# The opening of a hybrid decoder layer in another order: residual stream and query products first, memory tokens after them

## The chip, the cores and the metric

One core of one Trainium2 chip. The time is device microseconds of one execution of the whole kernel; lower is better. The kernel before took 2308.29 us, the median of three runs (2306.86 to 2318.2).

## The reference, cut to what matters

One layer on 512 tokens of width 2048, in float32. The change touches only what comes first: the embedding layer norm, a few columns of the input projection (gates, forget logits, the queries of the memory heads), and the keys and values of 256 memory tokens.

```
h = layer_norm(x, emb_ln_g, emb_ln_b)                 # x: 512 x 2048
proj = h @ w_in                                       # all heads' columns
moba_qkv, nsa_q, nsa_kv, nsa_g, fox_qkv, fox_f, mem_q = split(proj)
gates = sigmoid(nsa_g);  log_f = log_sigmoid(fox_f + b_forget)
ek, ev = split(mem @ w_mem_kv)                        # mem: 256 x 2048, 4 heads of 64 each
o_mem = softmax(mem_q @ ek.T / 8) @ ev
...                                                   # 28 more heads, output projection,
...                                                   # layer norm, gated MLP, layer norm
```

## The kernel before, in words

Every float32 product is made from two parts: an operand is rounded to a shorter type (the high part, by ScalarE) and the rest is kept as a low part (by VectorE, a subtraction). A product is then three matmuls: high by high, high by low, low by high (`PARTS`, line 118). All weights of a projection come in units of 128 x 1024 (512 KB): `load_unit` (line 88) loads one into a raw slot (tag `wr`, 4 slots), `nc.scalar.copy` makes the high part (line 99, tag `wh`, 2 slots) and `nc.vector.tensor_sub` the low part (line 100, tag `wl`, 2 slots). A tile of 128 output columns takes two units, that is 16 steps of 128 rows (`kt`) with three matmuls each (`gemm_t`, line 123).

The order of the instructions of each engine is written by a scheduler that follows the order of the program and moves an instruction up where its inputs are there. `high_priority(offset=n)` lets it act as if the instruction stood n places earlier; `self.ahead = 900` (line 1325) gives that to all units loaded after it. Attention of earlier heads is put into a queue and one stage of it is taken up by `tick` (line 141) for each so many columns of matmuls in `gemm_t`; `first_products` of the change does not count columns.

`build` (line 1293) opens in this order. The constants are made, and ScalarE's queue loads `prm` (line 182), a table of scales and offsets. The queue of SyncE (SP) then loads the memory tokens (`load_mem`, four tiles of 512 KB in tag `T`), the units of `w_mem_kv` and the residual stream x (`ln0_load`, sixteen tiles of 256 KB), mixed. `split_mem` splits the memory tokens; `mem_kv` makes four tiles of memory keys and values (tile `mkv`, 48 matmuls of 256 columns each, two units each), and between them `ln0_tile` normalises one token tile of x: `bn_stats` on VectorE (line 229), aggregation (lines 202 to 204), a power on GpSimd (line 205, engine POOL), the scale `nb` (line 233) and the normalisation itself, half on GpSimd (line 236), half on ScalarE (line 239).

`ln0_transpose` (line 241) then turns x: 4 transposes of 128 x 128 on TensorE per `kt` into a PSUM bank, and `evac_T` (line 208) takes it out by ScalarE (line 213, tile `ev`), GpSimd (the high part, line 215) and VectorE (the low part, line 216). The result, 16 tiles `T` of 128 x 1024, uses all 16 slots of tag `T`; in the kernel before the memory tokens, raw and split, hold 12 of these slots until the memory products are done. `fg` (line 425) makes gates and forget logits: its small weights are split side by side into one tile, so a `kt` takes two matmuls of 512 columns (line 437). `memory` (line 508) makes the two tiles of memory queries (`mq`, line 131) and queues the four memory heads. `fox` (first tile `fq`) follows.

`fg_stages` (line 443) is the first queued item. Its first stage is a chain of small steps on VectorE and ScalarE (lines 446 to 470), with two loads of ScalarE's function table, six GpSimd memsets and twelve small DMAs on SP's queue (line 478).

Of the kernel before, what the change touches and what calls it, by code (L numbers as in the profile page):

```python
# [11 lines left out]
F32 = mybir.dt.float32  # L12
F32R = mybir.dt.float32r
# [4 lines left out]
P = 128  # L18
S = 512
D = 2048  # L20
KT = D // P
NT = S // P
NMEM = 256
# [18 lines left out]
class Trunk:  # L42
# [176 lines left out]
    def ln0_load(self, t):  # L219
        self.xs.append([self.tmp(f"x{t}{n}") for n in range(4)])  # L220
        for n in range(4):
            self.nc.sync.dma_start(self.xs[t][n], self.x[t * P:(t + 1) * P, n * 512:(n + 1) * 512])

    def ln0_tile(self, t):
        nc = self.nc
# [196 lines left out]
        self.bias.append(b)  # L422


    def fg(self):

        nc = self.nc
        ps = self.bank("g", "fg")
        for u in range(2):
            raw = self.pW.tile([P, 8, 64], F32, tag="wr", name="wr", bufs=4)  # L430
            nc.sync.dma_start(raw, self.wfg[u])
            w = self.pW.tile([P, 8, P], F32R, tag="wh", name="wh", bufs=2)
            nc.scalar.copy(w[:, :, 0:64], raw)
            nc.vector.tensor_sub(w[:, :, 64:128], raw, w[:, :, 0:64].bitcast(F32))
            for k in range(8):
                for b in range(2):
                    nc.tensor.matmul(ps, w[:, k], self.xT_part(8 * u + k, b),
                                     start=(u + k + b == 0), stop=(u == 1 and k == 7 and b == 1))
        self.gates = self.cst.tile([P, NT, 24], F32, name="gates")
        self.crow = []  # L440
        self.queue.append(self.fg_stages(ps))

    def fg_stages(self, ps):
        nc = self.nc
# [47 lines left out]


    def load_mem(self, c):
        raw = self.pT.tile([P, 4, NMEM], F32, tag="T", name="mraw")
        self.nc.sync.dma_start(raw, self.memt[:, 4 * c:4 * c + 4, :])
        self.mraw.append(raw)

    def split_mem(self):
        for raw in self.mraw:  # L500
            h, l = (self.pT.tile([P, 4, NMEM], F32R, tag="T", name="mem") for _ in range(2))
            self.split_pair(raw, h, l)
            self.mt.append((h, l))

    def mem_kv(self, m, units):
        part = lambda kt, b: self.mt[kt // 4][b][:, kt % 4, :]
        ps = self.gemm_t(None, part, N=NMEM, units=units, name="mkv")
        return (self.stack_k if m < 2 else self.make_v)(ps, NMEM)

    def memory(self, kv):  # L510
        for c in range(2):
            qs = self.stack_q(self.wm_tile("mq"))
            oT = self.new_oT(14 + c)
            for h2 in range(2):
                self.queue.append(self.mem_head(qs[h2], kv[c][h2], kv[2 + c], h2, oT))
# [776 lines left out]

    def build(self):
        self.oT, self.bias = {}, []
        self.constants()

        self.xs, self.mraw, self.mt, kv = [], [], [], []
        unit = lambda m, u: self.load_unit(self.wmkv[m, u])

        def units(m, ahead):  # L1300
            with self.tc.high_priority(offset=ahead):
                return [unit(m, u) for u in range(2)]

        u0 = []
        for u in range(2):
            self.load_mem(2 * u)
            u0.append(unit(0, u))
            self.load_mem(2 * u + 1)
        self.ln0_load(0)
        u1 = units(1, 0)  # L1310
        for t in range(1, NT):
            self.ln0_load(t)
        self.split_mem()
        kv.append(self.mem_kv(0, u0))
        self.ln0_tile(0)
        u2 = units(2, 80)
        kv.append(self.mem_kv(1, u1))
        self.ln0_tile(1)
        self.ln0_tile(2)
        u3 = units(3, 0)  # L1320
        kv.append(self.mem_kv(2, u2))
        self.ln0_tile(3)
        kv.append(self.mem_kv(3, u3))
        self.ln0_transpose()
        self.ahead = 900
        self.fg()
        self.memory(kv)
        self.every = 23
        self.fox()
        self.every = 10  # L1330
        self.nsa_setup()
        for p in range(4):
            self.nsa_pair(p)
            self.moba_pair(p)
        self.out_proj()
        self.ffn()
# [91 lines left out]
```

## Time and profile before

| | |
|---|---|
| median of three runs | 2308.29 us |
| the profiled execution | 2307.26 us |
| its span, first to last instruction | 2305.2 us |
| TensorE (PE) matmuls busy | 2222.3 us, 96% |
| VectorE (DVE) | 1549.5 us, 67% |
| ScalarE (ACT) | 1234.9 us, 54% |
| GpSimd (POOL) | 1337.1 us, 58% |
| bytes by DMA | 392.74 MB, mean 170 GB/s |

The profile shows one execution. A busy share is the time in which an engine has an instruction in hand; matmuls overlap their neighbours, so the distance from start to start tells more of their rate than the duration. Times in rows are in us, means of groups in ns; "idle before" is the engine's idle time just ahead of these instructions and the arrow names what ended it. PEld is the loading of weights into TensorE; SPq and ACTq are the queues from which SyncE and ScalarE issue DMAs.

### The profile page before, as it was taken

The page shows a single profiled execution, that of the slowest core. Times are in us where ns is not written, and L with a number is a line of the kernel's source. Part 1 is how long each engine was busy: PE and PEld are TensorE (multiplying, and loading weights), DVE is VectorE, ACT ScalarE, POOL GpSimd, SP SyncE. Part 2 cuts the span into 40 slices and gives each one's busy share as a digit, 9 for nine tenths or more (in the row PEclk, how much of TensorE's full clock was granted, in tenths as well). Part 3 has the DMA queues.
Part 4 walks back from the last instruction along what each step waited for, and adds up shares of the span by engine and source line. Part 5 has one row for each costly group of instructions (what it writes and reads, how often), then busy time and mean ns, then how long its engine had stood idle before and what let it go on. Part 6 is the DMA issues. An engine that isn't in the chain of part 4 may idle for free. (4 is left out here: it accounts for less than half of the span.)

```text
span 2305.2 us, 40383 instructions
## 1 busy us (share of the span) xinstructions
PE 2222.3 (96%) x15454; PEld 2075.7 (90%) x15454; DVE 1549.5 (67%) x2212; ACT 1234.9 (54%) x2131; POOL 1337.1 (58%) x1199
## 2 busy tenths in 40 slices
PE   7999999999999998999999999999999899999995
PEld 6788888888888887899999999999999899999994
DVE  7544455466675338677776776776666987797878
ACT  5444443355564235665566566566656565665641
POOL 5212110133224706878787877888778677777675
PEclk9999999999999999999999999999999999999997
DMA  6322223221223453888888888888888888887963
GB/s 232 94 77 80 74 73 101 83 64 56 72 81 107 144 160 116 206 228 227 221 231 231 222 228 207 223 231 221 214 202 234 256 238 219 204 234 189 256 171 108
DMA packets 125362, 392.74 MB, mean 170 GB/s; under 512 B 13633, under 2 KB 23745, under 8 KB 125169
## 3 DMA queue, kind: packets, MB, share of 16 engines
q1 hardware_dynamic: 106304, 287.72, 37.6%
q0 software_dynamic: 18720, 102.24, 24.7%
q8 instruction: 121, 1.98, 0.3%
q14 instruction: 73, 0.59, 0.1%
q10 hardware_dynamic: 144, 0.21, 0.0%
HBM read 354.36 MB, written 35.65 MB: 169 GB/s over the span
## 5 line engine op out<-in xcount | busy, mean ns | idle before, releaser
L900 DVE TENSOR_TENSOR ws<-S,ws 128x512 fp32r<-128x512 f32 x512 | 621.5, 1233 | 245.6 <-ACT ws L899 242.3
L899 ACT CAST ws<-S 128x512 fp32r<-128x512 f32 x512 | 314.2, 614 | 140.2 <-PE up L977 57.9
L977 PE MATMUL up<-xt,ws 128*128 128x256 f32 x3096 | 386.4, 283 | 0.1
L977 PEld LDWEIGHTS up<-xt,ws 128*128 128x128 f32 x3096 | 378.0, 192 | 0.3 <-DVE ws L900 0.3
L100 DVE TENSOR_TENSOR wl<-wr,wh 128x1024 fp32r<-128x1024 f32 x122 | 154.7, 1268 | 213.7 <-ACT wh L99 192.1
L942 ACT CAST wh<-wr 128x512 fp32r<-128x512 f32 (+1 forms) x260 | 211.8, 831 | 136.8 <-PE up L977 135.0
L950 POOL TENSOR_TENSOR S<-wr 128x512 f32<-128x512 f32 x128 | 203.1, 1587 | 111.7 <-DVE ws L900 106.2
L342 POOL TENSOR_SCALAR P<-P,r 128x128 f32<-128x128 f32 (+3 forms) x144 | 81.2, 582 | 308.5 <-DVE r L337 166.1
L99 ACT CAST wh<-wr 128x1024 fp32r<-128x1024 f32 x122 | 128.0, 1049 | 236.1 <-PE op L733 78.7
L977 PE MATMUL up<-x,wh 128*128 128x256 f32 x1376 | 253.4, 284 | 0.0
L948 POOL TENSOR_TENSOR S<-wr 128x512 f32<-128x512 f32 x128 | 178.7, 1396 | 112.1 <-issue 68.4
L939 ACT ACTIVATE wl<-wr 128x512 fp32r<-128x512 f32 (+1 forms) x260 | 205.3, 837 | 66.8 <-PE dn L1154 55.6
L977 PEld LDWEIGHTS up<-x,wh 128*128 128x128 f32 x1376 | 216.2, 193 | 0.0
L951 POOL TENSOR_TENSOR S<-wr,S 128x512 f32<-128x512 f32 x128 | 212.1, 1657 | 0.0
L977 PE MATMUL up<-x,wl 128*128 128x256 f32 x688 | 196.3, 285 | 6.3 <-DMA wl<-in_wup_dram 6.3
L949 POOL TENSOR_TENSOR S<-S,wr 128x512 f32<-128x512 f32 x128 | 186.8, 1459 | 9.8
L1154 PE MATMUL dn<-wh,hx 128*128 128x256 f32 x792 | 158.3, 293 | 14.6 <-DVE acc L1167 5.9
L1154 PEld LDWEIGHTS dn<-wh,hx 128*128 128x128 f32 x792 | 132.6, 201 | 16.1 <-issue 6.4
L733 PE MATMUL op<-wh,oTs 128*128 128x512 f32 x448 | 140.7, 391 | 0.0
L977 PEld LDWEIGHTS up<-x,wl 128*128 128x128 f32 x688 | 133.1, 193 | 7.3 <-DMA wl<-in_wup_dram 7.3
L977 PE MATMUL up<-x,ws 128*128 128x256 f32 x1032 | 137.9, 283 | 0.0
L1154 PE MATMUL dn<-ws,hx 128*128 128x256 f32 x1044 | 134.1, 285 | 0.1
(331 smaller groups left out, 5143.3 us busy)
## 6 DMA issues: line engine op xcount, KB each, us to landing
wr<-in_wup_dram SPq DMA_DIRECT2D x176, 512.0 KB
wl<-in_wup_dram POOLq DMA_DIRECT2D x88, 768.0 KB, 7.4
wr<-in_wm_dram SPq DMA_DIRECT2D x84, 512.0 KB
wr<-in_wdown_dram SPq DMA_DIRECT2D x84, 512.0 KB
wl<-in_wdown_dram POOLq DMA_DIRECT2D x42, 768.0 KB, 7.8
wr<-in_wout_dram SPq DMA_DIRECT2D x32, 512.0 KB
hid<-c SPq DMA_DIRECT2D x44, 256.0 KB
hid<-ht SPq DMA_DIRECT2D x44, 256.0 KB
```

The lines of the kernel that those rows point to most:

```text
L100: nc.vector.tensor_sub(l[:, :cols], raw[:, :cols], h[:, :cols].bitcast(F32))
L733: nc.tensor.matmul(ps, ot[ct][:, a, t * P:(t + 1) * P], w[b][:, c2 * 512:(c2 + 1) * 512], start=(first and (a, b) == (0, 0)), stop=(last a ...
L899: ins = self.nc.scalar.copy(h, raw)
L900: self.nc.vector.tensor_sub(l, raw, h.bitcast(F32))
L939: nc.scalar.mul(l3[:, o], i, -1.0)
L942: nc.scalar.copy(h3[:, o], i)
L948: nc.gpsimd.tensor_add(s12[:, 0], a21, a22)
L949: nc.gpsimd.tensor_sub(s12[:, 1], s12[:, 0], a11)
L950: nc.gpsimd.tensor_sub(s34[:, 0], a11, a21)
L951: nc.gpsimd.tensor_sub(s34[:, 1], a12, s12[:, 1])
L977: self.nc.tensor.matmul(ps, w[iw][i][:, k * P:(k + 1) * P], x[j][ix], start=(opens and k == 0 and (i, j) == (0, 0)), stop=(last and k == 3 ...
L1154: self.nc.tensor.matmul(bk[i][:, a * 256:(a + 1) * 256], x[ix][j][:, a * P:(a + 1) * P], w[iw][p][:, q * 256:(q + 1) * 256], start=first a ...
```

## The change

The residual stream is loaded ahead of all, its sixteen tiles by turns on SP's and on ScalarE's queue. The constants follow, then the gate weights (`fg_weights`, now in four tiles of tag `w`, split from two raw slots) and the two units of the first query tile. All of x is normalised and turned, and `first_products` makes gates (two matmuls) and the first query tile (three) together, step by step. Only then the memory tokens are loaded, into raw weight slots (tag `wr`), split into sixteen small tiles of tag `t` in place of eight in tag `T`, and multiplied; the second query tile follows.

```
     def ln0_load(self, t):
         for n in range(4):
-            self.nc.sync.dma_start(self.xs[t][n], self.x[...])
+            eng = self.nc.scalar if n % 2 else self.nc.sync
+            eng.dma_start(self.xs[t][n], self.x[...])

-    def fg(self):
...
+    def fg_weights(self):
+        out = []
         for u in range(2):
             raw = self.pW.tile([P, 8, 64], F32, tag="wr", name="wr", bufs=4)
             nc.sync.dma_start(raw, self.wfg[u])
+            for i in (0, 4):
+                w = self.tmp("wfg", (P, 4, P), F32R, tag="w")
+                nc.scalar.copy(w[:, :, 0:64], raw[:, i:i + 4])
+                nc.vector.tensor_sub(w[:, :, 64:128], raw[:, i:i + 4],
+                                     w[:, :, 0:64].bitcast(F32))
+                out.append(w)
+        return out
+
+    def first_products(self, wfg, units):
+        pf, pq = self.bank("g", "fg"), self.bank("g", "gt")
+        for kt in range(KT):
+            for b in range(2):
+                nc.tensor.matmul(pf, wfg[kt // 4][:, kt % 4], self.xT_part(kt, b), ...)
+            u, k = divmod(kt, KT // 2)
+            for a, b in self.PARTS:
+                nc.tensor.matmul(pq, units[u][a][:, k * P:(k + 1) * P], self.xT_part(kt, b), ...)
+        self.wm_next = 1
         self.gates = self.cst.tile([P, NT, 24], F32, name="gates")
         self.crow = []
-        self.queue.append(self.fg_stages(ps))
+        self.queue.append(self.fg_stages(pf))
+        return self.stack_q(pq)

     def load_mem(self, c):
-        raw = self.pT.tile([P, 4, NMEM], F32, tag="T", name="mraw")
+        raw = self.pW.tile([P, 4, NMEM], F32, tag="wr", name="mraw", bufs=4)
         self.nc.sync.dma_start(raw, self.memt[:, 4 * c:4 * c + 4, :])
...
+        for i in (0, 2):
+            h, l = (self.tmp("mem", (P, 2, NMEM), F32R) for _ in range(2))
+            self.split_pair(raw[:, i:i + 2], h, l)
             self.mt.append((h, l))

-    def memory(self, kv):
+    def memory(self, kv, first):
         for c in range(2):
-            qs = self.stack_q(self.wm_tile("mq"))
+            qs = self.stack_q(self.wm_tile("mq")) if c else first
...
     def build(self):
+        for t in range(NT):
+            self.ln0_load(t)
         self.constants()
-        ...
+        wfg = self.fg_weights()
+        first = [self.load_unit(self.wm[0, u]) for u in range(2)]
+        for t in range(NT):
+            self.ln0_tile(t)
         self.ln0_transpose()
+        qs = self.first_products(wfg, first)
+        units = []
+        for c in range(4):
+            self.load_mem(c)
+            if c in (1, 3):
+                units.append(self.load_unit(self.wmkv[0, c // 2]))
+        kv = [self.mem_kv(0, units)]
+        for m in range(1, 4):
+            kv.append(self.mem_kv(m, [self.load_unit(self.wmkv[m, u]) for u in range(2)]))
         self.ahead = 900
-        self.fg()
-        self.memory(kv)
+        self.memory(kv, qs)
```

## Rows read from the trace of the kernel before

**Rows 1.** Stretches of the span: us, each engine's busy time, granted clock, DMA share, GB/s.
```profile
0.00:62.00 62.00, 45.28 (x291) 38.15 (x292) 46.23 (x74) 34.43 (x48) 31.58 (x41) 1.00 0.60 216
...
84.00:200.00 116.00, 115.95 (x565) 97.30 (x565) 61.67 (x108) 55.89 (x118) 26.18 (x44) 1.00 0.26 78
```

**Rows 2.** What TensorE waited for, first 62 us: total, times, longest.
```profile
PE mkv L131 <- ACT mem L899: 9.3, 1, 9.3
...
PE mkv L131 <- DVE wl L100: 2.7, 4, 1.2
...
PE mkv L131 <- ACT wh L99: 0.7, 1, 0.7
```

**Rows 3.** Order of time on TensorE: start, duration, instructions, idle before.
```profile
14.31 0.41 PE L131 MATMUL mkv<-mem,wl 128*128 128x256 f32 x1
...
14.95 0.41 PE L131 MATMUL mkv<-mem,wl 128*128 128x256 f32 x1
...
41.24 0.28 PE L131 MATMUL mkv<-mem,wl 128*128 128x256 f32 x1
...
41.60 0.28 PE L131 MATMUL mkv<-mem,wl 128*128 128x256 f32 x1
...
47.94 0.60 PE L174 MATMUL xTp<-ident,x 128*128 128x128 f32 x4
...
48.62 0.60 PE L174 MATMUL xTp<-ident,x 128*128 128x128 f32 x4
...
61.77 0.63 PE L131 MATMUL mq<-T,wh 128*128 128x512 f32 x2
...
83.83 0.62 PE L131 MATMUL fq<-T,wh 128*128 128x512 f32 x2
```

**Rows 4.** The first 28 us in two stretches, columns as in rows 1.
```profile
0.00:6.00 6.00, 0.00 (x0) 0.00 (x0) 0.33 (x6) 1.28 (x1) 3.91 (x13) 1.00 0.63 185
6.00:28.00 22.00, 16.32 (x109) 15.42 (x110) 18.55 (x30) 13.15 (x15) 6.09 (x6) 1.00 1.04 401
```

**Rows 5.** Groups by shape, first 62 us: count, busy us, mean ns, idle before.
```profile
L229 DVE BATCH_NORM_STATS2 st<-x 128x6 f32<-128x512 f32 x16 | 10.4, 678 | 0.1
...
L205 POOL TENSOR_TENSOR mu<-mu,mhalf 128x1 f32<-128x1 f32 x4 | 3.1, 779 | 22.5 <-DVE mu L204 22.3 <-DMA x<-in_x_dram 0.3
...
L236 POOL TENSOR_SCALAR x<-x,mu 128x512 f32<-128x512 f32 x8 | 9.0, 1135 | 0.4
...
L239 ACT ACTIVATE x<-x,nb,mu 128x512 f32<-128x512 f32 x8 | 6.1, 809 | 5.4 <-DVE nb L233 5.4
...
L202 DVE BATCH_NORM_AGGREGATE mv<-st 128x2 f32<-128x24 f32 x4 | 1.0, 257 | 0.0
...
L215 POOL TENSOR_SCALAR T<-ev 128x512 fp32r<-128x512 f32 x16 | 15.6, 999 | 3.9 <-ACT ev L213 3.9
...
L216 DVE TENSOR_TENSOR T<-ev,T 128x512 fp32r<-128x512 f32 x16 | 15.7, 1041 | 1.5 <-POOL T L215 1.5
...
L100 DVE TENSOR_TENSOR wl<-wr,wh 128x1024 fp32r<-128x1024 f32 x9 | 11.0, 1223 | 7.4 <-ACT wh L99 7.4
...
L99 ACT CAST wh<-wr 128x1024 fp32r<-128x1024 f32 x10 | 10.5, 1046 | 17.9 <-DMA wr<-in_wmkv_dram 10.4 <-PE fg L437 7.5
```

**Rows 6.** Order of time on SP's queue: the last raw slots, and the gate chain's DMAs.
```profile
26.64 4.65 SPq L431 DMA_DIRECT2D wr<-in_wfg_dram  x2
36.08 53.44 SPq L93 DMA_DIRECT2D wr<-in_wm_dram  x10
...
98.62 1.49 SPq L478 DMA_DIRECT2D crow<-cn  x2
```

**Rows 7.** Issues of x on SP's queue: ns min/median/max, first and last start.
```profile
L222 SPq DMA_DIRECT2D x<-in_x_dram x16: 327/328/480, 4.1 to 22.3; - x16
```

**Rows 8.** The gate chain's stretch, 77.22 to 92.40 us, columns as in rows 1.
```profile
77.22:92.40 15.18, 15.18 (x68) 12.57 (x68) 10.95 (x16) 8.45 (x10) 3.82 (x8) 1.00 0.29 92
```

**Rows 9.** Groups of VectorE in that stretch: the unit subtractions among them.
```profile
L100 DVE TENSOR_TENSOR wl<-wr,wh 128x1024 fp32r<-128x1024 f32 x3 | 3.6, 1193 | 0.0
```

More of the change, by code (lines that the diff above doesn't have):

```diff
@@ L221, in ln0_load @@
         for n in range(4):
-            self.nc.sync.dma_start(self.xs[t][n], self.x[t * P:(t + 1) * P, n * 512:(n + 1) * 512])
+            eng = self.nc.scalar if n % 2 else self.nc.sync
+            eng.dma_start(self.xs[t][n], self.x[t * P:(t + 1) * P, n * 512:(n + 1) * 512])
     def ln0_tile(self, t):
@@ L422, in alibi @@
         self.bias.append(b)
-    def fg(self):
+    def fg_weights(self):
         nc = self.nc
-        ps = self.bank("g", "fg")
+        out = []
         for u in range(2):
@@ L431, in fg @@
             nc.sync.dma_start(raw, self.wfg[u])
[L432 to L438, printed above, removed]
+            for i in (0, 4):
[6 more added lines that the diff above has]
+    def first_products(self, wfg, units):
+        nc = self.nc
+        pf, pq = self.bank("g", "fg"), self.bank("g", "gt")
+        for kt in range(KT):
+            for b in range(2):
+                nc.tensor.matmul(pf, wfg[kt // 4][:, kt % 4], self.xT_part(kt, b),
+                                 start=(kt + b == 0), stop=(kt == KT - 1 and b == 1))
+            u, k = divmod(kt, KT // 2)
+            for a, b in self.PARTS:
+                nc.tensor.matmul(pq, units[u][a][:, k * P:(k + 1) * P], self.xT_part(kt, b),
+                                 start=(kt == 0 and (a, b) == (0, 0)),
+                                 stop=(kt == KT - 1 and (a, b) == (1, 0)))
+        self.wm_next = 1
         self.gates = self.cst.tile([P, NT, 24], F32, name="gates")
         self.crow = []
-        self.queue.append(self.fg_stages(ps))
+        self.queue.append(self.fg_stages(pf))
+        return self.stack_q(pq)
     def fg_stages(self, ps):
@@ L494, in load_mem @@
     def load_mem(self, c):
-        raw = self.pT.tile([P, 4, NMEM], F32, tag="T", name="mraw")
+        raw = self.pW.tile([P, 4, NMEM], F32, tag="wr", name="mraw", bufs=4)
         self.nc.sync.dma_start(raw, self.memt[:, 4 * c:4 * c + 4, :])
[L497 to L502, printed above, removed]
+        for i in (0, 2):
+            h, l = (self.tmp("mem", (P, 2, NMEM), F32R) for _ in range(2))
+            self.split_pair(raw[:, i:i + 2], h, l)
             self.mt.append((h, l))
     def mem_kv(self, m, units):
-        part = lambda kt, b: self.mt[kt // 4][b][:, kt % 4, :]
+        part = lambda kt, b: self.mt[kt // 2][b][:, kt % 2, :]
         ps = self.gemm_t(None, part, N=NMEM, units=units, name="mkv")
         return (self.stack_k if m < 2 else self.make_v)(ps, NMEM)
-    def memory(self, kv):
+    def memory(self, kv, first):
         for c in range(2):
-            qs = self.stack_q(self.wm_tile("mq"))
+            qs = self.stack_q(self.wm_tile("mq")) if c else first
             oT = self.new_oT(14 + c)
@@ L1294, in build @@
         self.oT, self.bias = {}, []
+        self.xs, self.mt = [], []
+        for t in range(NT):
+            self.ln0_load(t)
         self.constants()
[L1297 to L1323, printed above, removed]
-        self.ln0_transpose()
+        wfg = self.fg_weights()
+        first = [self.load_unit(self.wm[0, u]) for u in range(2)]
+        for t in range(NT):
+            self.ln0_tile(t)
+        self.ln0_transpose()
+        qs = self.first_products(wfg, first)
[7 more added lines that the diff above has]
+            kv.append(self.mem_kv(m, [self.load_unit(self.wmkv[m, u]) for u in range(2)]))
         self.ahead = 900
-        self.fg()
-        self.memory(kv)
+        self.memory(kv, qs)
         self.every = 23
```

## The prediction, made before the changed kernel was run

> **What bounds the kernel now.** I read the stretches of the span first [rows 1]. After the opening's 62 us the matmuls fill nearly every microsecond (115.95 of 116.00 from 84 to 200 us). The change moves no instruction that lies behind the first `fq` tile, and it adds or drops no matmul. So whatever it brings is brought before that tile's first matmul, at 83.83 us [rows 3]; later stages shift as a block. Of these two stretches the opening is the one with holes: 45.28 of 62.00 us.
>
> What TensorE waits for there comes next [rows 2]: 9.3 us until the first memory product can start, 2.7 and 0.7 us between weight units of the memory products. A hole need not be a wait, though, so the order of time is read too [rows 3]. Three numbers come out of it. Three memory matmuls of 256 columns take 0.64 us early on (14.31 to 14.95) and 0.36 us later (41.24 to 41.60): 768 columns at the 1.2 GHz level first, near the 2.4 GHz level after, although the granted-clock column reads 1.00 throughout; the full pace came after 14.95, some 6 us behind the first product at 9.3. A round of four transposes and one gate matmul takes 0.68 us (47.94 to 48.62). And 96 query matmuls take 22.06 us (61.77 to 83.83, two small transposes among them), 0.23 us each or 10.9 us a tile. Between 41.6 and 61.77 us TensorE waits on the making of the `T` tiles: GpSimd 999 ns and VectorE 1041 ns a tile, in step with each other [rows 5].
>
> **The change, part by part.** I follow TensorE from the start to the first `fq` matmul and compare with 83.83 us.
>
> *When x is there.* x is 512 x 2048 x 4 bytes, 4.19 MB. The first 6 us move 6 x 185 KB = 1.1 MB, and then 401 GB/s flow [rows 4], so x is all in at 6 + 3.1/0.401 = 13.7 us, and I take 14.0 with its completion. ScalarE issues eight of the loads, at 0.33 us each [rows 7] 2.6 us, ahead of its `prm` load; it has nothing else to do before the first token tile is measured. SP's sixteen issues, 5.2 us of work, were spread from 4.1 to 22.3 us [rows 7]: an issue can be held by transfers ahead of it. If ScalarE's are, it is held until some 10 us, when only the first token tile waits for it, for 2 to 3 us. I cost that at nothing, since the last tile sets the end. `prm` is needed at 18 us and has 4 us to spare.
>
> SP's queue, nearly alone, holds the DMA engines at a share of 1.04 from 6 us on, but at 0.63 before that [rows 4]. If a second queue filled that ramp from 2 us on, x would be in at 2 + 4.19/0.401 = 12.4 us, 1.3 us sooner; if not, 13.7. I take the latter, since at 0.33 us an issue [rows 7] SP alone puts out 256 KB tiles at 0.8 MB a us, twice what flows. The Trainium skill, "DMA: Bandwidth & Descriptors", section "Issuing engines are not separate DMA queues", says that issuing from several engines saves only the time to issue; by that rule the sum stays as I have it, by the other reading it is 1.3 us less.
>
> *When the transposes start.* After the last load come two `bn_stats` (2 x 0.68), an aggregation (0.26), the power (0.78), three steps on one or two columns (0.2 each by my estimate, below the aggregation) and ScalarE's normalisation (0.81) [rows 5]: 3.8 us, so 17.8. GpSimd has two normalisations of 1.1 and a power for each token tile, near 3.1 us a tile against 2.6 us of loading, so it runs late, and the splits of the gate weights and the first query units are on the same engines: I take **18.0**, bounds 17 to 20. Before, TensorE began at 9.28: here the change loses 8.7 us.
>
> *Transposes, gates and first queries together.* The first product follows the first transposes by ScalarE's evacuation (0.8 us, as long as its normalisation of the same size) and GpSimd's 1.0 us [rows 5] plus the transposes: 20.3. A `kt` then costs TensorE 0.45 us of transposes (0.68 less one matmul of 0.23) and five matmuls of 0.23, 1.59 us; that is over the 1.04 us of VectorE's step, so **TensorE is the bound in place of the evacuation**, and the 16 `kt` take 25.4 us. About three banks of transposes are done before 20.3 (less 1.35), and if the full pace comes 6 us after the first transposes, as before after the first product, 1.8 us are lost to the half level. End: 20.3 + 25.4 - 1.35 + 1.8 = **46.2**. The gate products ended at about 61.8 before.
>
> *Memory tokens later.* 4 tiles x 16 steps x 0.36 = 23.0 us at full pace: all of it now, where before part ran at the half level. Tokens and first unit are loaded and split under the stage above. There VectorE has 16 subtractions (11 us without GpSimd in its way, 16.7 with), eight small token splits and three units (1.22 each): under 28 us in either case, so I cost them at nothing; if they were late, the first memory product would wait for up to a load and a split, 4 us. What stays is the hand-over from unit to unit. There are two `wh`/`wl` pairs, and a pair is free when TensorE has done with its unit; then come 1.05 us on ScalarE and 1.22 on VectorE [rows 5], 2.4 with signals, against 24 x 0.12 = 2.88 us of matmuls of the other unit. The room is 0.5 us. Before, with bn_stats between, the hand-overs cost 2.7 + 0.7 = 3.4 us [rows 2]. Now it is the gate chain that lies between: `tick` comes up at the end of the first memory tile. Its steps hold VectorE for some 7.3 us (10.95 busy less three units of 3.6) [rows 8, 9], ScalarE for its casts and two table loads, SP for twelve small DMAs (1.49 us for the last two), ahead of unit loads [rows 6], and GpSimd for six memsets. Before, they lay under query products, where a unit lasts 5.5 us. Below, the gaps can be nothing; above, each of seven hand-overs waits 1.4 us, some 10. I take **4.0**, near the old value, since VectorE's load is alike. End: 46.2 + 23.0 + 4.0 = 73.2.
>
> *Second query tile* 10.9, and 0.5 us of value transposes: **84.6**. Against 83.83 that is +0.8 us. The tick for gates, done earlier, moves one stage of attention ahead; that work lies under full matmuls [rows 1] and is costed at nothing.
>
> The sum for the profiled execution is 2307.26 + 0.8 = 2308.1; the median of the runs shown lies 1.03 above it, so I forecast **2309.0**. In short, 8.7 us of later start eat what the shared stage wins: before, 41.6 to 61.8 us held 14.6 us of work (16 rounds of 0.45 and 32 matmuls of 0.23), 5.6 us less than it took, and the rest is small items of both signs.
>
> **The rivals.**
> *The covers hold (faster, but little).* Transposes at 17.0, full clock at once after them, gaps of 0.5: 84.6 - 1 - 1 - 3.5 = 79 us, so 2303 to 2304. For it: the residual stream has the DMA engines to itself. Against it: the hand-over room of 0.5 us with 7.3 us of gate steps inside. Even with no gap at all the opening is 18 + 25.4 + 23 + 10.9 = 77.3 us, 6.5 below 83.83, so the opening alone cannot reach 0.5% (11.5 us).
> *The gate chain starves the memory products.* Gaps of 10: 2315. For it: VectorE would have 7.3 us of gate steps and 1.22 for each 2.88 us unit at once, nearly full. Against it: the chain itself waits on ScalarE's table loads and leaves holes.
> *One pair for the memory products (slower).* The second query tile's first unit has a look-ahead of 900. If it takes a `wh`/`wl` pair while six memory units are still to come, each of these waits its whole split, 2.4 us, behind the unit before it: 6 x 2.4 = 14.4, and 2 more where a gate step stands ahead of it, in place of 4: 2321, +0.55%. It decides only if all six units are so caught; three would give 2314. Against it: before, the gate weights without look-ahead kept their raw slots ahead of query units with it [rows 6], at 26.64 against 36.08.
> *It does not do what it says.* The scheduler may put memory products among the first ones; both pairs are held by the first query units until half of them are done, so that this changes little: 2307 to 2310.
> *A later stage is laid out differently* by a moved start, by 12 us or more either way: nothing in the rows speaks for it.
>
> **How the numbers follow.** About 0.5% is what a measurement of this kernel can tell (the runs shown span 11 us). Forecast or the like of it, including the case that it does not do what it says, 0.50; covers hold 0.22; starved 0.16; one pair, or a mishap of its price, 0.07; later stage 0.05, 0.03 of it faster. The first three all lie within 0.5%: same 0.88; faster 0.03; slower 0.09. The range takes in the covers' 2303 with 3 us for a measurement, and the starved case's 2315 with the same: 2300 to 2318. It leaves out one pair and the later stage.
>
> **What the changed profile would show.** x all loaded at 14 us, transposes starting at 17 to 20, `xTp`, `fg` and the first query matmuls in one stretch that ends at 45 to 48 with TensorE near full; memory products from there, waits of 2 to 6 us on VectorE's `wl` or ScalarE's `wh`; `fq` starting at 80 to 89 us. A start of transposes after 22, memory products waiting over 10 us, or a first `fq` matmul below 77 us would make the prediction wrong, and so would a stretch after 100 us whose busy time differs by more than 3 us.

## The result, and the profile after

The change makes the kernel **slower by 0.7%**: 2324.07 us (median of 7 runs) against 2306.86 beside it (7 runs), ratio 1.007, 95% interval 1.0057 to 1.0084, or some 13 to 19 us. The profiled execution took 2327.36 us; its span is 2325.3 us against 2305.2, at a mean granted clock of 0.984 against 0.988. The opening accounts for it: the first `fq` matmul stands at 102.42 us, against 83.83 before [rows 3] and 84.6 in the forecast; from there to the end of the span 2222.9 us pass, against 2221.4 before.

The changed kernel's opening by stretches: bounds and length in us, busy time (and instructions) of PE, PEld, DVE, ACT and POOL, granted clock of TensorE, DMA share, GB/s.

```profile
0.00:27.75 27.75, 5.95 (x24) 4.27 (x24) 16.43 (x45) 12.11 (x18) 13.64 (x27) 1.00 0.83 291
27.75:50.50 22.75, 22.75 (x120) 19.13 (x120) 16.72 (x17) 10.34 (x15) 14.95 (x15) 1.00 0.08 24
50.50:53.35 2.85, 0.19 (x1) 0.00 (x0) 1.34 (x2) 1.85 (x4) 1.76 (x3) 1.00 0.00 0
53.35:62.10 8.75, 5.88 (x30) 5.18 (x30) 8.25 (x13) 6.17 (x10) 4.01 (x8) 0.76 0.61 199
62.10:68.10 6.00, 5.96 (x28) 5.96 (x29) 2.93 (x5) 3.49 (x5) 0.00 (x0) 0.50 0.68 236
68.10:79.80 11.70, 11.26 (x92) 10.90 (x91) 9.98 (x13) 6.19 (x9) 0.00 (x0) 1.00 0.44 134
79.80:82.58 2.78, 0.05 (x1) 0.00 (x0) 1.67 (x3) 1.75 (x3) 0.00 (x0) 0.85 0.59 190
82.58:88.50 5.92, 5.92 (x27) 5.92 (x28) 0.83 (x2) 1.30 (x3) 0.00 (x0) 0.50 0.35 104
88.50:91.06 2.56, 2.56 (x23) 2.56 (x23) 1.22 (x1) 0.49 (x1) 0.00 (x0) 0.98 0.03 6
91.06:102.42 11.36, 11.36 (x54) 9.41 (x53) 3.21 (x4) 2.94 (x6) 0.00 (x0) 1.00 0.48 141
```

These rows answer to [rows 1]. Until 27.75 us TensorE does 24 transposes and no product. Transposes and the joint products (gates and first query tile) then run without a hole to 50.5. Another hole follows, and the memory products, 23.0 us of work at full pace, take from 53.35 to 91.06. In three of their stretches the granted clock is far below 1.00, at 0.50 in two: the 1.2 GHz level. What TensorE waited for in this opening (total, times, longest; the waits above 0.5 us):

```profile
PE xTp L174 <- ACT x L240: 14.0, 1, 14.0
PE xTp L174 <- POOL x L237: 7.5, 2, 6.9
PE mkv L131 <- DVE tk L277: 2.7, 1, 2.7
PE mkv L131 <- ACT mem L913: 2.7, 1, 2.7
PE mkv L131 <- ACT wh L99: 1.5, 1, 1.5
PE pg L174 <- DVE fg L464: 0.9, 1, 0.9
```

Each hole is followed into the order of time of the engine that ended it (start, duration, engine, line, operation, tiles, count, idle time before and its releaser). First ScalarE, from the last normalisations to the tokens:

```profile
16.22 0.71 ACT L435 CAST wfg<-wr 128x256 fp32r<-128x256 f32 x2 [2.27 <-DMA wr<-in_wfg_dram]
...
19.43 0.81 ACT L240 ACTIVATE x<-x,nb,mu 128x512 f32<-128x512 f32 x1
...
24.80 1.52 ACT L240 ACTIVATE x<-x,nb,mu 128x512 f32<-128x512 f32 x2 [0.51 <-DVE nb L234]
...
50.73 0.59 ACT L259 ACTIVATE q<-gt 64x512 fp32r<-64x512 f32 x1 [8.19 <-PE gt L451]
52.07 0.59 ACT L259 ACTIVATE q<-gt 64x512 fp32r<-64x512 f32 x1 [0.75 <-DVE q L260]
52.69 4.26 ACT L913 CAST mem<-mraw 128x512 fp32r<-128x512 f32 x8
...
79.77 1.04 ACT L99 CAST wh<-wr 128x1024 fp32r<-128x1024 f32 x1 [1.52 <-PE mkv L131]
80.84 0.76 ACT L276 CAST tk<-mkv 64x256 fp32r<-64x256 f32 x2
```

The instructions stand in the order in which the scheduler wrote them, and an instruction that waits keeps those behind it waiting. At 13.95 us ScalarE has normalised one piece of x and then waits 2.27 us for gate weights, which it has to cast first. At 42.5 us it falls idle for 8.19 us: the token casts stand behind the evacuations of the query tile, which is not finished. At 78.25 it waits for a weight slot, and the evacuation of a key tile (`tk`), whose bank TensorE needs, stands behind. VectorE in the first of these places:

```profile
14.78 1.28 DVE L230 BATCH_NORM_STATS2 st<-x 128x6 f32<-128x512 f32 x2
16.66 2.31 DVE L436 TENSOR_TENSOR wfg<-wr,wfg 128x256 fp32r<-128x256 f32 x4 [0.60 <-ACT wfg L435]
...
19.06 0.63 DVE L230 BATCH_NORM_STATS2 st<-x 128x6 f32<-128x512 f32 x1
19.61 1.20 DVE L100 TENSOR_TENSOR wl<-wr,wh 128x1024 fp32r<-128x1024 f32 x1
...
21.46 1.20 DVE L100 TENSOR_TENSOR wl<-wr,wh 128x1024 fp32r<-128x1024 f32 x1
...
22.65 0.68 DVE L230 BATCH_NORM_STATS2 st<-x 128x6 f32<-128x512 f32 x1
```

Thirteen of the sixteen statistics are done by 16.1 us; the last three are spread to 23.3 by splits of gate and query weights. And TensorE's order shows the price of a hole after it has ended:

```profile
54.54 0.63 PE L131 MATMUL mkv<-mem,wh 128*128 128x256 f32 x2
...
55.18 0.63 PE L131 MATMUL mkv<-mem,wh 128*128 128x256 f32 x2
...
68.21 0.40 PE L131 MATMUL mkv<-mem,wh 128*128 128x256 f32 x2
...
68.57 0.40 PE L131 MATMUL mkv<-mem,wh 128*128 128x256 f32 x2
```

Three memory matmuls take 0.64 us after the hole and 0.36 later, the two paces of [rows 3]. The slow one runs from 54.5 to 57.7, 62.1 to 68.1 and 82.6 to 88.5: 15.1 us, of which 15.1 x 0.28/0.64 = 6.6 are lost.

### The profile page after: what moved, and what is told of

Same layout as the page of the kernel before. It is cut to its first block, busy times and chain, and to the rows that moved or that the text cites. A ratio compares the mean times of both kernels' runs of the same rounds, so it can differ in the third digit from the quotient of the medians.

```text
span 2325.3 us, 40392 instructions
## 1 busy us (share of the span) xinstructions
PE 2224.9 (96%) x15454; PEld 2082.3 (90%) x15454; DVE 1564.8 (67%) x2218; ACT 1236.4 (53%) x2137; POOL 1333.4 (57%) x1199
## 5 line engine op out<-in xcount | busy, mean ns | idle before, releaser
L914 DVE TENSOR_TENSOR ws<-S,ws 128x512 fp32r<-128x512 f32 x512 | 634.5, 1259 | 231.6 <-ACT ws L913 226.0
L264 POOL TENSOR_SCALAR q<-q 64x512 fp32r<-64x512 f32 x64 | 45.7, 715 | 174.6 <-ACT q L259 120.8
```

What stands on the lines that cost most here:

```text
L914: self.nc.vector.tensor_sub(l, raw, h.bitcast(F32))
```

## The experiments

The measure of the opening is the start of the first `fq` matmul; 102.42 in the changed kernel, 83.83 before. How far it can be trusted is shown by one kernel profiled twice (the sixth and twelfth run below): 84.88 and 85.75, while its spans were 2304.6 and 2310.7. So a difference of 1 us at `fq` is about what one profile can tell, and the time of a single execution says little here; ratios are given only for kernels run in five rounds.

**1. Normalise first.** Weights are split after x in the order of the code.

```
-        wfg = self.fg_weights()
-        first = [self.load_unit(self.wm[0, u]) for u in range(2)]
         for t in range(NT):
             self.ln0_tile(t)
+        wfg = self.fg_weights()
+        first = [self.load_unit(self.wm[0, u]) for u in range(2)]
```

> Edit: in the order of the program the normalisation of x stands ahead of the splits of the gate weights and of the first query units; nothing else moves. Theory (splits in front): in the changed kernel VectorE measures the last token tiles only after 2.3 us of gate-weight and 2.4 us of query-unit subtractions and the waits for their loads, so the last tile is normalised at 25.6 us and the first gate product starts at 27.75. Then here the last normalisation ends near 19, the first product starts at 20 to 22 and the first fq matmul comes at 95 to 97 us in place of 102.4; the time of the run is 5 to 7 us under the changed kernel's. Rival (x arrives late, by its two queues or behind held issues on ScalarE): all of these stay within 1.5 us of the changed kernel's.

`fq` at 101.43: the theory's number is missed. The last normalisation does come earlier, at 21.04 instead of 24.80, but ScalarE then does the weight casts ahead of its first evacuation (its order of time):

```profile
21.04 1.52 ACT L240 ACTIVATE x<-x,nb,mu 128x512 f32<-128x512 f32 x2 [0.62 <-DVE nb L234]
22.46 1.31 ACT L435 CAST wfg<-wr 128x256 fp32r<-128x256 f32 x4
23.68 1.99 ACT L99 CAST wh<-wr 128x1024 fp32r<-128x1024 f32 x2
25.57 8.79 ACT L213 ACTIVATE ev<-xTp,prm 128x512 f32<-128x512 f32 x13
```

The splits were moved from one place on the path to the next. The first product came at 32.9, with 56 of the 64 transposes ahead of it, and the last joint product ended at 52.2 us, against 50.7 in the changed kernel.

**2. Tokens early.** Tokens are loaded and split ahead of the joint products in the order of the code, and the first memory units after them.

```
-        qs = self.first_products(wfg, first)
         for c in range(4):
             self.load_mem(c)
-            if c in (1, 3):
-                units.append(self.load_unit(self.wmkv[0, c // 2]))
+        qs = self.first_products(wfg, first)
+        units = [self.load_unit(self.wmkv[0, u]) for u in range(2)]
```

> Edit: the memory tokens are loaded and split ahead of the first products in the order of the program, and the first memory units right after them. Theory (the splits of the tokens stand behind the first query tile's evacuation, and hold the raw slots of the next units): start of the first product as in the changed kernel (27.75), but the memory products follow the first products at 50.5 without the wait of 2.7 us and without the wait of 1.55 us for a late unit; the two stretches at half level behind those waits (53.4 to 57.7 and 62.1 to 68.1, some 5 us lost) go too. First fq matmul at 92 to 96 us. Rival (the hand-overs of two weight pairs beside the gate chain bind whatever the tokens do): the waits move to later units and fq comes at 99 to 102.

`fq` at 96.06, 6.4 earlier. The waits for `mem` are gone, and so is the half level behind them: the granted clock is 1.00 from 50 to 70 us. The wait for `tk` is still there, now 3.9 us, and 2.3 us of waits for weight splits (`wl`) have appeared beside it.

**3. Gate chain late.** `fg_stages` is queued after the memory products instead of ahead of them.

```
-        self.queue.append(self.fg_stages(pf))
+        self.pf = pf
...
         self.ahead = 900
+        self.queue.append(self.fg_stages(self.pf))
```

> Edit: the gate chain is put into the queue behind the memory products, so that no stage of it is taken up inside them. Theory (the gate chain on VectorE and ScalarE delays the evacuation of the first key tile, for whose bank the fourth memory tile waits 2.73 us, and puts the clock to its half level from 82.6 to 88.5): that wait, the half level behind it and the 0.9 us wait of the gate transposes go, fq at 95 to 98 us; waits for the tokens stay. Rival (the two weight pairs bind, not the chain): waits on wh or wl of the same sum appear in its place, fq at 100 to 103.

`fq` at 95.16, 7.3 earlier: a hit. The wait for `tk`, the one for the gates' `fg`, and the last half-level stretch are gone; the wait of 2.7 us for `mem` stays.

**4. Waits filled.** Eighteen matmuls whose result nobody uses are put ahead of the fourth memory tile; the scheduler ran twelve in the wait for `tk` and six in two others.

> Edit: 18 matmuls of 512 columns whose result nobody reads are added ahead of the fourth memory tile, 12 of them in its wait (2.73 us), 5 in an earlier wait of 1.55 us and one between; nothing is left out. Theory (half level after a wait: TensorE's clock is at 1.2 GHz from 62.1 to 68.1 and from 82.6 to 88.5 us because it stood idle just before): with the waits filled the memory matmuls behind them run at 0.36 us for three in place of 0.64, so the last memory matmul comes 3 to 6 us sooner and fq at 96.5 to 99.5 us, although TensorE has 4.1 us more to do. Rival (the half level comes from something else, or is worth nothing since the next unit is waited for anyway): fq at 102 to 106.

`fq` at 99.53, 2.9 earlier with 4.1 us of work more and a first product that came 1.3 later. The stretches that ran at 0.50 in the changed kernel:

```profile
62.10:68.10 6.00, 6.00 (x45) 5.52 (x44) 4.39 (x8) 4.71 (x7) 0.00 (x0) 1.00 0.87 320
68.10:79.80 11.70, 10.63 (x86) 10.27 (x85) 9.96 (x13) 6.10 (x8) 0.00 (x0) 1.00 0.47 141
79.80:88.50 8.70, 8.70 (x63) 7.92 (x62) 3.72 (x5) 3.48 (x7) 0.00 (x0) 1.00 0.45 129
```

The idle time ahead, not the memory products, is what lowers the clock.

**5. Both mended** (2 and 3 together).

> The changed kernel with both single mends together: tokens loaded and split ahead of the first products, gate chain queued behind the memory products. Theory (two waits in different places of the opening, each with its own half-level stretch): the gains add, 102.42 - 6.4 - 7.3 = 88.7 for the first query product of the fox stage, between 87 and 91; the wait on the token split at 50 us and the wait for the evacuated key tile at 73 to 79 us are both gone, and what is left against the kernel before (83.83) is the late first product, some 5 us. Time: the kernel before plus 3 to 8 us, ratio 1.001 to 1.0035. Rival (both waits hide one later bound, the loads of the memory weights): 94 to 96, no better than either alone, with longer waits on the weight splits, ratio 1.005.

`fq` at 86.0, ratio 1.0023 (1.0009 to 1.0037): a gain of 16.4 us where 6.4 and 7.3 add to 13.7, and so better than the theory's 87 to 91: each mend alone left the other wait, which in run 2 grew from 2.7 to 3.9 us. No memory product waits more than 0.2 us, and the clock stays at 1.00. The first product is as late as ever, at 28.0.

**6 and 12. Weights first.** As 5, with one queue for x and the gate and query weights loaded and split ahead of x.

> As the kernel with both mends, but the 1.5 MB of gate and first query weights are loaded and split ahead of x, and x is issued by SyncE alone. Theory (the first product is late because weight splits stand between the statistics of x on VectorE, and the statistics themselves fill VectorE): the weights delay x by 3.9 us and then cost nothing more; last normalisation 24 to 26 us, first product 26 to 28.5 us, first query product of the fox stage within 2 us of the kernel with both mends. Rival (weight splits alone made it late): last normalisation at 18 to 21.5, first product by 23.5, and the fox stage 4 us earlier than with both mends, 83 to 86.

> The kernel with the gate and query weights ahead of x, one queue for x, tokens early and the gate chain late, timed in rounds. Theory (the opening ends at 84.85 against 83.83, and nothing after it differs but by the planner's order): ratio 0.9995 to 1.0015. Rival (the later stages, that came out 1.6 us shorter in its one profile, are shorter for a reason): ratio 0.997 to 0.9995.

First product at 26.9 in both, last normalisation at 23.87, `fq` at 84.88 and 85.75: the theory's numbers. In rounds 1.0012 (0.9998 to 1.0026).

**7. Joint products in the old order.** The kernel before with `fg_weights`, `first_products` and `stack_q` of the change, put where `fg` stood.

```
-        self.fg()
-        self.memory(kv)
+        wfg = self.fg_weights()
+        first = [self.load_unit(self.wm[0, u]) for u in range(2)]
+        self.memory(kv, self.first_products(wfg, first))
```

> The kernel before with one part of the change alone: gate products and first query tile made together in one round of 16 steps, memory products first as before. Theory: the 16 rounds that wait for evacuations of x from 41.6 to 61.8 us take up the 10.9 us of the query tile's products in their idle time: stage from 41.6 to 64 or so, then the second query tile, first query product of the fox stage at 76 to 80 instead of 83.83, time 2299 to 2304 against 2307 of the kernel before, ratio 0.9965 to 0.999. Rival (the splits of the gate and query weights stand in front of the evacuations on ScalarE and VectorE, as they did in the changed kernel with normalisation first): the stage begins 4 to 6 us later, fox at 82 to 86, ratio 0.999 to 1.001.

`fq` at 79.7, ratio 0.998 (0.9969 to 0.9991): faster than both kernels. Its stretches from the joint products on:

```profile
45.40:68.30 22.90, 22.71 (x119) 19.09 (x120) 17.02 (x17) 10.22 (x15) 14.71 (x15) 1.00 0.19 63
68.30:79.70 11.40, 11.40 (x52) 9.38 (x52) 4.16 (x5) 3.55 (x5) 2.94 (x4) 1.00 0.30 92
```

The query products fill the holes of the rounds that waited for the tiles `T`. TensorE's wait for them, in the kernel before and then here:

```profile
PE fg L437 <- DVE T L216: 3.0, 8, 1.0
```

```profile
PE fg L446 <- DVE T L216: 0.2, 1, 0.2
```

**8. One queue.** The changed kernel with all of x issued by SyncE.

```
-            eng = self.nc.scalar if n % 2 else self.nc.sync
-            eng.dma_start(self.xs[t][n], ...)
+            self.nc.sync.dma_start(self.xs[t][n], ...)
```

> The changed kernel with the second queue undone: all sixteen tiles of x issued by SyncE. Theory (the DMA engines, not the issuing engine, set the pace of x, and ScalarE's held issues cover no work that matters, since VectorE's statistics set the pace): bandwidth in the first 6 us within 10 of 184 GB/s, first query product of the fox stage within 1.5 us of 102.42. Rival 1 (ScalarE kept from normalising until 11.84 us is what makes the last token tile late): first product 2 to 4 us earlier, fox at 98 to 100.5. Rival 2 (the second queue does fill the start): x later by 1 us or more, fox at 103.5 or later.

The theory fell. First product at 24.2 instead of 27.75, `fq` at 97.2. ScalarE's order:

```profile
10.74 1.52 ACT L239 ACTIVATE x<-x,nb,mu 128x512 f32<-128x512 f32 x2 [4.70 <-DVE nb L233]
...
18.68 1.31 ACT L434 CAST wfg<-wr 128x256 fp32r<-128x256 f32 x4
19.97 1.52 ACT L239 ACTIVATE x<-x,nb,mu 128x512 f32<-128x512 f32 x2
```

With one queue the statistics of the first token tile are put together at 7.63 us (10.04 with two), and six of ScalarE's eight normalisations stand ahead of the weight casts (one with two). Rival 1's number for the first product came out, its number for `fq` did not (97.2 is below its 98), and that ScalarE was held by its issues is not shown by it: the scheduler's order changed with the queue. Of the 5.2 us at `fq`, 2.1 are there when the joint products end (48.6 against 50.7); the rest comes in the memory products, and no cause was sought.

**9. Both mended and one queue** (5 with 8).

> The changed kernel with both mends (tokens early, gate chain late) and with x on one queue. Theory (the second queue costs 3.5 us of the first product, 27.75 to 24.2, by itself, and nothing hides that here): 86.0 - 3.5 = 82.5 for the first query product of the fox stage, between 81 and 84.5, level with 83.83 of the kernel before; ratio 0.999 to 1.0015. Rival (the memory stage, once mended, takes up the late start, since its weights arrive when they do): 85.5 to 87, new waits on the weight splits, ratio 1.0015 to 1.003.

`fq` at 83.7, ratio 1.0 (0.9988 to 1.0013). Theory again, if less than its 82.5: the joint stage took 24.8 us, 2 more than in the changed kernel, and it began at half pace (matmuls of 512 columns start 0.42 us apart at 24.74 and 25.16; at full pace 0.23). Joint products, memory products and query tile:

```profile
24.10:48.90 24.80, 24.80 (x121) 20.76 (x121) 22.80 (x26) 15.32 (x24) 15.52 (x15) 1.00 0.37 118
48.90:72.30 23.40, 23.40 (x194) 23.21 (x193) 12.99 (x14) 11.31 (x15) 2.95 (x4) 1.00 0.63 200
72.30:83.70 11.40, 11.40 (x54) 9.46 (x54) 3.21 (x4) 2.92 (x6) 0.00 (x0) 1.00 0.46 139
```

With three causes taken out, the new order is level with the old one, not better.

**10. Queue by token tile.** The changed kernel with `t % 2` for `n % 2`: tiles 0 and 2 by SyncE.

> The changed kernel with x still on two queues, but split by token tile and not by piece: tiles 0 and 2 by SyncE, 1 and 3 by ScalarE. Theory A (a tile's statistics need all four of its pieces, and the two queues that share each tile finish it late): the first tile is complete by 7.5 to 9 us as with one queue (7.63), the last normalisation starts by 21.5 and the first product by 25.5; fox stage at 97 to 100. Theory B (ScalarE is held by its own issues until 11.8 us and its normalisations fall behind the casts of the weights): first tile complete early but first normalisation on ScalarE not before 11.8, first product at 26.5 to 28.5, fox at 100.5 to 103.

Neither theory's start: the first tile's statistics were put together at 11.31, ScalarE's first normalisation came at 16.2, the first product at 30.0, `fq` at 102.1. SyncE's issues of weights now stood between its two tiles of x, so the order had changed once more; the run cannot tell the two apart.

**11. Two queues in the old order.** The kernel before, with x on two queues and nothing else.

> The kernel before with one part of the change alone: x issued half by SyncE and half by ScalarE. Theory (ScalarE's issues are held by earlier transfers, and its casts of tokens and weights for the memory products wait behind them): the first memory product, 14.31 before, or a later one waits 1 to 4 us longer, first query product of the fox stage at 84.5 to 88. Rival (DMA is the bound and issues cost nothing): within 0.7 us of 83.83. Rival 2 (SyncE's 0.33 to 0.48 us an issue held the tokens and weights back): 81.5 to 83.1.

`fq` at 82.1: rival 2. The theory is wrong here too: in the old order the second queue costs nothing, and may bring 1.7 us.

**13. Weights between.** As 8 (one queue), with the gate and query weights loaded between token tiles 1 and 2. It was to part what 8 and 10 left together, the queue and the place of the splits.

> The changed kernel with one queue for x, and the gate and query weights loaded between token tiles 1 and 2. Theory (the place of the weight splits among the statistics and normalisations of x makes the first product late, not the second queue as such): some splits stand ahead of the last statistics again, last normalisation on ScalarE starts at 22 to 25.5 against 19.97 with x ahead of all on one queue, first product at 25.5 to 28.5 against 24.2. Rival (late pieces and held issues of the second queue): with one queue no such delay but that of 1.5 MB of weights for the second half of x, which lands where the statistics still work off the first half; last normalisation by 21.5, first product at 23.5 to 25.

Last normalisation at 25.12, first product at 28.1, `fq` at 101.9, with one queue: the theory's numbers. VectorE, ScalarE's last normalisations, and SyncE's queue:

```profile
17.32 1.59 DVE L100 TENSOR_TENSOR wl<-wr,wh 128x1024 fp32r<-128x1024 f32 x1
18.84 2.46 DVE L229 BATCH_NORM_STATS2 st<-x 128x6 f32<-128x512 f32 x4
```

```profile
25.12 1.52 ACT L239 ACTIVATE x<-x,nb,mu 128x512 f32<-128x512 f32 x2 [0.63 <-DVE nb L233]
```

```profile
8.61 6.36 SPq L222 DMA_DIRECT2D x<-in_x_dram  x8
```

Eight statistics are done here when the splits begin, thirteen in the changed kernel; in both the rest stands behind them. But the place of the splits is not all that differs from run 8: the last issue of x ends at 14.97 us here and at 10.89 there, so x itself comes some 4 us later, and most of the 5.1 us at the last normalisation can be that. Run 6 had the same weights ahead of the last of x, with the splits ahead of all statistics but one, and its first product came at 26.9. So some 1.2 us are left for the place of the splits, and the run alone does not show that it made the first product late.

**14. Joint products and two queues in the old order** (7 with 11).

> The kernel before with two parts of the change: gate products and first query tile made together, and x on two queues; memory products first. Theory (the two gains of 4.1 and 1.7 us at the fox stage lie in different stretches, the evacuation-bound products and the normalisation ahead of them): 77 to 79 against 79.7 with the joint products alone, ratio 0.9965 to 0.9985. Rival (both shorten the same wait, the first products' on the evacuated tiles of x, of which 0.2 us is left with the joint products): 79 to 80.5, ratio 0.9975 to 0.9995.

`fq` at 78.5, the theory's number, but the ratio is 0.9987 (0.9973 to 1.0001), which does not part it from 7 or from no change. That the second queue gains time is not shown.

## Why the prediction was wrong

The bound was read rightly: only the opening counts. Over the kernels run in rounds the shift of `fq` and that of the time (ratio less one, times 2307) go together: +18.6 and +16.1 for the change, +2.2 and +5.3 (run 5), +1.9 and +2.8 (run 12), -0.1 and 0.0 (run 9), -4.1 and -4.6 (run 7), -5.3 and -3.0 (run 14), each shift inside its interval. So later stages do "shift as a block". The miss is inside the opening, 102.42 - 84.6 = 17.8 us, by its own steps:

- **"I take 18.0, bounds 17 to 20"** for the transposes, and 20.3 for the first product: 27.75, so +7.45. (The transposes of the tiles that were ready began at 14.01; the last tile's, which this step is about, could not before 24.8.) Two terms failed. One is the arrival of x, "I take 14.0". ScalarE's last issue stood at 11.4 us, and an issue needed at least 5.1 us to land, so that x was not all in before 16.5, 2.5 us late:

```profile
L223 ACTq DMA_DIRECT2D x<-in_x_dram x8: 334/335/453, 1.2 to 11.4; - x8
...
DMA to landing us min/median/max: 5.1/5.8/6.5
```

  The other is the way from the last load to the last normalisation on ScalarE: 3.0 us in the forecast's chain, 8.3 here (16.5 to 24.80). The forecast named the splits "on the same engines" without pricing them. They went ahead of the last statistics and normalisations, 2.31 + 2 x 1.20 us on VectorE, with waits for their casts, which on ScalarE wait for their loads. Runs 1 and 8, with the splits behind the statistics, show it: 3.5 us (x in at some 17.5, normalised from 21.04) and 3.7 (16.2 and 19.97), near the forecast's 3.0. But in both the casts then stood ahead of evacuations: run 8 got its first product at 24.2, and run 1 gained nothing by the end of the joint products.
- **The second queue "at nothing"**. Undone, it gives back 3.5 us of the first product. The transfers are not the reason, since the last of x lands at 16.2 with one queue and at 16.5 with two; as far as the runs tell it is the scheduler's order. The held issues themselves were not tested apart from it. Run 1 kept two queues and put x first: last normalisation 21.04, against 19.97 with one queue, so the late pieces cost some 1.1 there.
- **Joint stage, 25.9 us forecast:** 22.75, so -3.15. Most of the 1.8 for the half level did not come (the first `fg` matmuls already go at full pace; in run 9 it did come), and 24 transposes, not 12, were done before it.
- **Token splits "at nothing"**: +2.85, the hole from 50.5 to 53.35. VectorE had room under the joint stage (16.72 of 22.75 us busy), but the tokens' casts are on ScalarE, and their place there is behind the query tile. "If they were late" named 4 us; it was the case.
- **Memory products, 23.0 + 4.0:** 37.71, so +10.71. The waits came to 6.1, inside the bounds of 0 to 10, if for other reasons: 2.7 for `tk` and 0.9 for the gates' evacuation were no hand-over of units. What no step had is **the half level after a hole**, 6.6 us. The forecast knew both paces and used the slow one once, at the start. Of the remaining 2.0 no cause was sought.
- **Second query tile:** 11.36 against 11.4, so -0.04.

7.45 - 3.15 + 2.85 + 10.71 - 0.04 = 17.82. The nearest rival, the starved memory products, had the place right and the price too small, because it counted waits only. The rival of one weight pair did not occur.

That a second queue would not fill the first microseconds was right. The changed kernel's first stretch, against 185 GB/s and a share of 0.63 in [rows 4]:

```profile
0.00:6.00 6.00, 0.00 (x0) 0.00 (x0) 1.03 (x7) 0.00 (x0) 1.17 (x8) 1.00 0.65 184
```

The rule of the Trainium skill that the forecast weighed ("DMA: Bandwidth & Descriptors", section "Issuing engines are not separate DMA queues") is borne out by it. It also says that the time to initiate a transfer is usually small beside the transfer. The trace agrees for the single issue, 0.33 to 0.45 us against at least 5.1 us to landing; but ScalarE's eight issues were spread from 1.17 to 11.75 us, and it did no other work in between.

The idea of sharing the stage was sound. In the old order, where the memory products cover the normalisation, it gains 0.2%; in the new order TensorE has nothing to do until x is normalised, and even run 9 only comes out level.

## What to carry to other kernels

When work is moved, write down for each engine what stands ahead of it in its queue, not only how much the engine has to do: the last statistics, the token casts and the key tile's evacuation were all short instructions behind others that waited for something else. Count when the last load lands, not only how fast the bytes flow: here that was 2.5 us more. Price a hole on TensorE with the stretch after it at half pace, which here cost 6.6 us on top of 8.9 us of holes (2.85 and 6.1). And filling the holes of a bound stage with other products is worth trying apart from any reordering: that part alone beat both kernels.

## What was not expected of the hardware

The clock fell after short holes: to 0.50 after 2.66 us of idle time (from 54.5, the hole ended at 53.35), after one of 0.93 and one of 1.55 (62.1), and after 2.73 (82.6); after the 0.44 at 74.1 it did not. In the kernel before, the matmuls behind single holes of 0.95 us (at 19.82) and 1.19 us (at 30.99) went at the full pace too. And which engine issues a load changed more than the load: with x on two queues the first token tile was measured later (10.04 us) than with one (7.63), at much the same flow (184 GB/s against 205 in the first 6 us, 373 against 358 in the next 8), and the order of splits and statistics changed with it.
